# Additions of output parts on GpSimd, ordered behind the scaling of probabilities

## The chip, the core and the metric

The kernel runs on one core of a Trainium2 chip. The metric is device time in microseconds (us) of one execution; less is better. The core has engines that each work through a queue of instructions in order: TensorE (PE; its weight loads are listed apart, as PEld), VectorE (DVE), ScalarE (ACT) and GpSimd (POOL). SyncE (SP) issues DMAs, and so do some of the others.

## The reference

One inference step of a two-layer streaming encoder in fp32, on 1024 prompt tokens and on 8 running streams of 16 new tokens each. Width 1024, 16 query heads of 64 in 4 groups that share a key/value head, MLP width 4096. The first layer's mixer is windowed attention with its own keys and values; the second layer's attends to a shared pair. The change lies in the second, of which the core is:

```python
def attend(q, k, v, bias, sink):                  # sink is None in the second layer
    qg = q.reshape(b, tq, N_KV_HEADS, GROUP, HEAD_DIM)
    s = jnp.einsum('bqhgd,bkhd->bhgqk', qg, k) * (HEAD_DIM ** -0.5)
    s = s + bias.reshape(N_KV_HEADS, GROUP, tq, -1)   # learned bias on clipped distance, band mask
    p = jax.nn.softmax(s, axis=-1)
    return jnp.einsum('bhgqk,bkhd->bqhgd', p, v).reshape(b, tq, N_HEADS * HEAD_DIM)

# second layer, prompt (hp) and running streams (hs) alike
qp = project_q_b(hp, g_attn[layer], w_q_b[j], g_q_b[j])     # RMSNorm, projection, norm of each head
ap = band_attention_prompt(qp, kb_p, vb_p, LEFT_CHUNKS_B, rel_fn, None)  # own chunk of 64 + 8 before
hp = hp + ap @ w_o_b[j]
hp = hp + jnp.square(jax.nn.relu(rmsnorm(hp, g) @ w_up)) @ w_down
```

## The kernel before

**Tiles and halves.** Tokens are cut into tiles of 128: eight of the prompt, numbered 0 to 7, and a ninth, ST, that holds the running streams. The attention of the second layer has two halves: the first takes key/value heads 0 and 1 (query heads 0 to 7) over tiles 0 to 7, the second heads 2 and 3 over the same tiles. One step is a group (tile, key/value head). A float32 matrix product is made of three products of a high and a low part: `split` (L128 to L134) casts the high part and subtracts it to get the low one.

**One group.** A query projection (L217 to L219) reads the normed residual's parts hh and hl from DRAM (hTd), norms and turns it (L238, L239, L260). The scores of a group are stated two groups ahead of its use. PE makes them against up to five tiles of keys (L431; `ps_sf` the far keys, `ps_sn` the near ones), DVE takes minima and adds the bias (L455 to L459), ACT makes the exponentials with their sums (L468, L471), DVE the reciprocals li (L478), and POOL scales each 128x640 row block p by li (L481, two at a time; `score_w` does the same for tiles 2 and 3 at L526). Later PE turns p (L324), ACT and DVE split it into pth and ptl (L128, L134), PE multiplies by the values into `ps_pv` (L331, L332), and `pv_store` copies the result and stores it to DRAM (oTd) in two parts (v = 0 and 1), each of 64 of the 128 rows of `ps_pv`, whose sum is the output.

**Output projection.** `WO(t, half)` (from L1580) brings a tile's output of one half back: `load_halves` loads part 0 into o and part 1 into o2 on SP (L337, L339), and GpSimd adds them in place (L341). Buffers o and o2 come from a scratch pool of two. A split gives oh (cast on POOL, L130) and ol (subtraction on DVE, L134). Then eight pieces of three matmuls each (L176 to L178) go into `ps_mm`, one PSUM bank; DVE adds the residual (L1614), and a DMA stores the tile to xd, on SP's queue for the first half, on POOL's for the second. The pieces are fill work: a plan by hand says at which of the 32 groups a tile's projection is stated, and between the steps of attention a piece at a time is set. Tiles 0 to 5 of the first half are stated at groups 15, 17, 19, 21, 23 and 25, ST at 27, 7 at 28 and 6 at 29; of the second half 0, 4 and 1 at 31, 5, 2 and 3 at 32. These make 14 additions on POOL: eight of the first half, six of the second. The second half of tiles 6, 7 and ST is projected after the attention (`ps_wo`), with the additions on DVE. Tiles 0 and 4 stay in SBUF and are normed there (L641), ordered behind a mark at the last reciprocal. Then come norms, turns of the normed tiles (`ps_n`, L690) and the MLP's matmuls (L743 to L745).

**Decode units.** The running streams' attention is set in small units between the groups (L568 to L615: memset pn, `ps_utp`, `ps_uo`).

**What sets the order.** The code is stated in the order above, and a scheduler then lists every engine's instructions by a model of their times (`TC_KW = dict(schedule_with_timeline_sim=True)`); the engines run those lists in order. So an instruction that is stated early may be listed later on its engine, and with another dependence the list of every engine can come out otherwise. A method adds an order by hand, a dependence on the scheduler's list that is no semaphore:

```python
    def behind(self, a, b):
        self.tc.add_manual_dep(b.ins, a.ins.name, AFTER, reason="order")
```

In the first layer the two parts are not kept apart (its setting `o2` is 0), so it has no such additions.

Of the kernel before, what the change touches and what calls it, by code (L numbers as in the profile page):

```python
# [11 lines left out]
ALU = mybir.AluOpType  # L12
# [82 lines left out]
class Build:  # L95
# [238 lines left out]
    def load_halves(self, layer, half, t, a, b, e=None):  # L334
        nc = self.nc
        src = self.oTd[layer][half][t]
        nc.sync.dma_start(a, src[:, 0])  # L337
        if self.o2[layer] and t < NT:
            nc.sync.dma_start(b(), src[:, 1])  # L339
            e = e or (nc.gpsimd if self.o2[layer] == 1 else nc.vector)  # L340
            e.tensor_tensor(a, a, self.last, ALU.add)  # L341

    def pv_store(self, apool, pv, dst, j):
        nc = self.nc
# [21 lines left out]
    def score_a(self, apool, small, t, j, qT, probs):  # L366
        nc = self.nc
# [6 lines left out]
        p = apool.tile([P, G, 256], F32, tag="p", name="p", bufs=self.pb)  # L374
        for i2 in range(0, G, 2):
# [7 lines left out]
            for i in range(i2, i2 + 2):  # L383
                h = j * G + i
# [8 lines left out]
            for i in range(i2, i2 + 2):  # L393
                h = j * G + i
# [5 lines left out]
                yield  # L400
        li = self.sink_norm(small, nm, self.sink[:, j * G : j * G + G], l, G)
        for i in range(G):
            nc.gpsimd.tensor_scalar(
                p[:, i, 0:W], p[:, i, 0:W], li[:, i : i + 1], 1.0, ALU.mult, ALU.mult
            )
        probs[t, j] = p
# [12 lines left out]
    def score_b(self, apool, small, t, j, qT, probs):  # L419
        nc = self.nc  # L420
# [6 lines left out]
        li = small.tile([P, G], F32, tag="li", name="li")  # L427
# [8 lines left out]
        for i2 in range(0, G, 2):  # L436
# [13 lines left out]
            for i in range(2):  # L450
                h = j * G + i2 + i
# [10 lines left out]
            for i in range(2):  # L462
                h = i2 + i
                p = apool.tile([P, 640], F32, tag="p", name="p", bufs=self.pb)
# [13 lines left out]
            nc.vector.reciprocal(li[:, h2], l[:, h2, 1])  # L478
            for h in range(i2, i2 + 2):
                p = ps[h][:, : nk * P]  # L480
                nc.gpsimd.tensor_scalar(p, p, li[:, h : h + 1], 1.0, ALU.mult, ALU.mult)  # L481
            if i2 == 0:
                yield
        probs[t, j] = ps
# [1 line left out]
    def score_w(self, apool, small, t, j, qT, probs):  # L486
        nc = self.nc
# [6 lines left out]
        li = small.tile([P, G], F32, tag="li", name="li")  # L494
        for i2 in range(0, G, 2):
# [18 lines left out]
            for i in range(2):  # L514
                h = i2 + i
                p = apool.tile([P, 640], F32, tag="p", name="p", bufs=self.pb)
# [6 lines left out]
            nc.vector.reciprocal(li[:, h2], l[:, h2])  # L523
            for h in range(i2, i2 + 2):
                p = ps[h][:, 0:W]
                nc.gpsimd.tensor_scalar(p, p, li[:, h : h + 1], 1.0, ALU.mult, ALU.mult)  # L526
            if i2 == 0:
                yield
        probs[t, j] = ps
# [1376 lines left out]
```

## Time and profile before

| what | value |
|---|---|
| median of 3 runs (lowest, highest) | 2359.23 us (2354.69, 2363.7) |
| the profiled execution: time, span | 2354.01 us, 2352.2 us |
| granted TensorE clock, mean over the span | 0.997 |
| busy: PE, PEld | 2271.4 us (97%), 1893.3 us (80%) |
| busy: DVE, ACT, POOL | 1715.4 us (73%), 1332.4 us (57%), 635.3 us (27%) |

Busy time and spans come from the profile of one execution; the instructions that only issue DMAs or handle semaphores are not counted as busy. In rows of groups, `out<-in` names the tiles, `x14` the count, then busy time, mean ns of one, idle time of the engine just before the group and what ended it. In rows by time the columns are start, duration, engine, line, operation, and in brackets the wait ahead of it and its releaser. A row of waits is engine, tile and line `<-` releaser: us, count, longest. A row of stretches is window, length, busy time with count of PE, PEld, DVE, ACT and POOL, granted clock, busy share of the DMA engines, GB/s. A row of DMA issues ends with KB each and the median us from issue to landing.

### The profile page before, as it was taken

The numbers are of one execution on the slowest core, as the hardware profiler recorded it, in microseconds if no ns is written. First come the engines' busy times: TensorE is split into PE (matmuls) and PEld (weight loads), VectorE is DVE, ScalarE is ACT, GpSimd is POOL, SyncE is SP. The second block draws the span as 40 slices with busy tenths as digits, with TensorE's granted clock in tenths as the row PEclk, the third lists the DMA queues.
The fourth block names the chain that finished last, engine by engine and source line by source line (L and its number), as shares of the span: only waits on it lengthen the run. The fifth ranks groups of instructions, "written<-read, shape, count | busy, mean of one in ns | idle before, by whom it ended". The sixth has DMA issues, their size and how long they took to land.

```text
span 2352.2 us, 33396 instructions
## 1 busy us (share of the span) xinstructions
PE 2271.4 (97%) x11429; PEld 1893.3 (80%) x11429; DVE 1715.4 (73%) x3075; ACT 1332.4 (57%) x2684; POOL 635.3 (27%) x950
## 2 busy tenths in 40 slices
PE   7998999899999999999999999998899999999999
PEld 6787887788888888777877788887788888888787
DVE  6788786766656578899577877777666566678987
ACT  3777674655555555344377666665655555565443
POOL 4334332313213111002333434344132132110011
PEclk9999999999999999999999999999999999999999
DMA  7335546234434677748653655555244343977567
GB/s 253 127 113 163 171 147 202 95 122 160 137 111 151 218 230 177 267 147 214 183 157 113 193 157 177 174 168 184 69 156 138 113 162 107 284 209 199 175 169 192
DMA packets 226715, 392.70 MB, mean 167 GB/s; under 512 B 51592, under 2 KB 126288, under 8 KB 226448
## 3 DMA queue, kind: packets, MB, share of 16 engines
q1 hardware_dynamic: 188816, 283.58, 37.4%
q0 software_dynamic: 36432, 102.26, 15.9%
q10 hardware_dynamic: 1296, 4.72, 0.5%
q8 instruction: 90, 1.47, 0.2%
q14 instruction: 81, 0.66, 0.1%
HBM read 236.51 MB, written 156.85 MB: 167 GB/s over the span
## 4 chain that ended last, share of the span: by engine, by line
PE 74%; DVE 9%; DMA 9%; ACT 3%; issue 3%; POOL 1%; SPq 0%; ACTq 0%; DVEq 0%; POOLq 0%
PE ps_c L743 6%; PE ps_c L744 6%; PE ps_c L745 6%; PE ps_x L743 5%; PE ps_x L745 5%; PE ps_x L744 5%; PE ps_mm L217 3%; PE ps_mm L219 3%; PE ps_mm L218 3%; PE ps_y L745 2%; PE ps_y L743 2%; PE ps_y L744 2%; PE ps_tr L324 2%; DMA a<-hd 2%; DVE w L134 1%
## 5 line engine op out<-in xcount | busy, mean ns | idle before, releaser
L744 PE MATMUL ps_c<-w,a 128*128 128x512 f32 x960 | 374.7, 390 | 6.9 <-DVE w L134 6.9
L743 PE MATMUL ps_c<-w,a 128*128 128x512 f32 x960 | 375.1, 391 | 5.1 <-DVE x L1174 3.1
L745 PE MATMUL ps_c<-w,a 128*128 128x512 f32 x960 | 374.3, 390 | 0.0
L908 POOL DMA_DIRECT2D hd<-h x272 | 148.9, 550 | 594.8 <-ACT h L817 378.2
L743 PEld LDWEIGHTS ps_c<-w,a 128*128 128x128 f32 x960 | 180.6, 188 | 46.3 <-issue 4.7
L744 PEld LDWEIGHTS ps_c<-w,a 128*128 128x128 f32 x960 | 180.7, 188 | 46.1 <-DVE w L134 9.0
L745 PEld LDWEIGHTS ps_c<-w,a 128*128 128x128 f32 x960 | 180.5, 188 | 37.5
L128 ACT CAST a<-a 128x1536 fp32r<-128x1536 f32 x80 | 118.6, 1482 | 149.5 <-DMA a<-hd 149.5
L217 PE MATMUL ps_mm<-w,hh 128*128 128x512 f32 x432 | 172.7, 401 | 8.8 <-POOL w L185 3.3
L134 DVE TENSOR_TENSOR a<-a 128x1536 fp32r<-128x1536 f32 x80 | 140.5, 1756 | 45.7 <-ACT a L128 45.7
L219 PE MATMUL ps_mm<-w,hl 128*128 128x512 f32 x432 | 171.7, 398 | 1.5 <-DMA hl<-hTd 1.4
L218 PE MATMUL ps_mm<-w,hh 128*128 128x512 f32 x432 | 170.8, 396 | 1.3 <-DVE w L190 1.1
L743 PE MATMUL ps_x<-sx,w 128*128 128x512 f32 (+1 forms) x408 | 157.8, 387 | 3.7 <-ACT h L864 2.7
L128 ACT CAST w<-s 128x2048 fp32r<-128x2048 f32 x56 | 107.1, 1912 | 92.2 <-DVE s L1060 80.7
L128 ACT CAST w<-ru 128x512 fp32r<-128x512 f32 (+1 forms) x160 | 110.0, 708 | 83.9 <-PE ps_y L744 32.0
L745 PE MATMUL ps_x<-sx,w 128*128 128x512 f32 (+1 forms) x408 | 154.1, 378 | 0.0
L744 PE MATMUL ps_x<-sx,w 128*128 128x512 f32 (+1 forms) x408 | 154.1, 378 | 0.0
L134 DVE TENSOR_TENSOR w<-s,w 128x2048 fp32r<-128x2048 f32 x56 | 128.1, 2288 | 32.4 <-ACT w L128 32.3
L1179 POOL DMA_DIRECT2D xp<-o x28 | 36.3, 1296 | 411.8 <-ACT o L1162 390.2
L134 DVE TENSOR_TENSOR ptl<-ps_tr,pth 128x512 fp32r<-128x512 f32 x180 | 122.4, 685 | 24.1 <-ACT pth L128 18.2
L134 DVE TENSOR_TENSOR w<-ru,w 128x512 fp32r<-128x512 f32 (+1 forms) x160 | 126.6, 793 | 14.7 <-ACT w L128 14.6
L816 ACT ACTIVATE h<-h 128x512 f32<-128x512 f32 (+1 forms) x102 | 61.9, 607 | 122.6 <-DVE h L866 93.5
(274 smaller groups left out, 6131.4 us busy)
## 6 DMA issues: line engine op xcount, KB each, us to landing
a<-hd SPq DMA_DIRECT2D x80, 768.0 KB, 6.2
hd<-h POOLq DMA_DIRECT2D x272, 192.0 KB, 2.5
ru<-in_w_up SPq DMA_DIRECT2D x64, 512.0 KB, 3.9
r<-in_w_down SPq DMA_DIRECT2D x32, 1024.0 KB, 10.0
xp<-o POOLq DMA_DIRECT2D x28, 768.0 KB, 9.4
o<-oTd SPq DMA_DIRECT2D x50, 256.0 KB, 5.0
x<-xp SPq DMA_DIRECT2D x23, 512.0 KB, 5.2
xp<-xo SPq DMA_DIRECT2D x18, 512.0 KB, 2.8
```

Of the source, the lines that this page charges most:

```text
L128: a = nc.scalar.copy(hi, src)
L134: return a, e.tensor_tensor(lo, src, hi.bitcast(F32), ALU.subtract)
L217: nc.tensor.matmul(ps, a, w[:, 0, k, :], start=(k == 0), stop=False)
L218: nc.tensor.matmul(ps, a, w[:, 1, k, :], start=False, stop=False)
L219: self.lp = nc.tensor.matmul(ps, b, w[:, 0, k, :], start=False, stop=(k == KC - 1))
L324: self.lp = nc.tensor.transpose(pt[:, i, :], get(i), self.ident)
L743: a = mm(ps, ah, bh, start=first, stop=False, skip_group_check=True)
L744: mm(ps, ah, bl, start=False, stop=False, skip_group_check=True)
L745: return a, mm(ps, al, bh, start=False, stop=last, skip_group_check=True)
L816: a = nc.scalar.activation(t, src, AF.Relu)
L908: return lambda p, z: self.nc.gpsimd.dma_start(self.hd[c // 4][:, p, c % 4], z)
L1179: nc.gpsimd.dma_start(dst, z, accum_op=ALU.add)
```

## The change

`load_halves` orders the addition behind `self.pl` where it is on GpSimd and of the first half. `self.pl` is the scaling of probabilities stated last: the three loops that scale on GpSimd set it. Eight additions are tied so (tiles 0 to 7 of the first half); the six of the second half on GpSimd and those on DVE are not. The scheduler then lists all engines anew.

```diff
@@ load_halves
         if self.o2[layer] and t < NT:
             nc.sync.dma_start(b(), src[:, 1])
-            e = e or (nc.gpsimd if self.o2[layer] == 1 else nc.vector)
-            e.tensor_tensor(a, a, self.last, ALU.add)
+            if e is None and not half:
+                self.behind(self.pl, nc.gpsimd.tensor_tensor(a, a, self.last, ALU.add))
+            else:
+                (e or nc.gpsimd).tensor_tensor(a, a, self.last, ALU.add)
...
@@ score_b (score_a and score_w alike)
             for h in range(i2, i2 + 2):
                 p = ps[h][:, : nk * P]
-                nc.gpsimd.tensor_scalar(p, p, li[:, h : h + 1], 1.0, ALU.mult, ALU.mult)
+                self.pl = nc.gpsimd.tensor_scalar(p, p, li[:, h : h + 1], 1.0, ALU.mult, ALU.mult)
```

From L342 on, line numbers of the changed kernel are two higher. Both kernels hold the same instructions. The lists are alike up to the first addition on POOL and again from the first matmuls of the second layer's MLP.

POOL's list around the first addition (tile 0), before:

```order
L481 TENSOR_SCALAR p_13624<-p_13624,li_13552 128x640
L481 TENSOR_SCALAR p_13627<-p_13627,li_13552 128x640
L341 TENSOR_TENSOR o_14133<-o_14133,o2_14135 128x512
L130 CAST oh_14138<-o_14133 128x512
L481 TENSOR_SCALAR p_13785<-p_13785,li_13766 128x640
L481 TENSOR_SCALAR p_13788<-p_13788,li_13766 128x640
L583 MEMSET pn_14096 128x128
L238 TENSOR_TENSOR qrs_14322<-qms_14320,mhalf_68 128x8
L481 TENSOR_SCALAR p_13847<-p_13847,li_13766 128x640
```

and in the changed kernel:

```order
L483 TENSOR_SCALAR p_13959<-p_13959,li_13940 128x640
L483 TENSOR_SCALAR p_13962<-p_13962,li_13940 128x640
L483 TENSOR_SCALAR p_14019<-p_14019,li_13940 128x640
L483 TENSOR_SCALAR p_14022<-p_14022,li_13940 128x640
L341 TENSOR_TENSOR o_14133<-o_14133,o2_14135 128x512
L585 MEMSET pn_14473 128x128
L130 CAST oh_14138<-o_14133 128x512
L483 TENSOR_SCALAR p_14176<-p_14176,li_14157 128x640
L483 TENSOR_SCALAR p_14179<-p_14179,li_14157 128x640
L238 TENSOR_TENSOR qrs_14322<-qms_14320,mhalf_68 128x8
```

The addition stood behind p_13627 and stands behind p_14022 now; the eight scalings from p_13785 to p_14022 have moved ahead of it.

PE's list where the projection of tile 0 begins (the first row with oh), before:

```order
L260 MATMUL ps_q<-identr,qr 128x128 x4
L431 MATMUL ps_sn<-KT,qT 128x256 x4
L331 MATMUL ps_pv<-pth,VS 128x512
L332 MATMUL ps_pv<-ptl,VS 128x512
L324 MATMUL ps_tr<-identr,p 128x128 x4
L331 MATMUL ps_pv<-pth,VS 128x512
L176 MATMUL ps_mm<-w,oh 128x512
L177 MATMUL ps_mm<-w,oh 128x512
L178 MATMUL ps_mm<-w,ol 128x512
```

and in the changed kernel:

```order
L331 MATMUL ps_pv<-pth,VS 128x512
L324 MATMUL ps_tr<-identr,p 128x128 x4
L332 MATMUL ps_pv<-ptl,VS 128x512
L260 MATMUL ps_q<-identr,qr 128x128 x4
L331 MATMUL ps_pv<-pth,VS 128x512
L176 MATMUL ps_mm<-w,oh 128x512
L177 MATMUL ps_mm<-w,oh 128x512
L332 MATMUL ps_pv<-ptl,VS 128x512
L324 MATMUL ps_tr<-identr,p 128x128 x4
L331 MATMUL ps_pv<-pth,VS 128x512
L433 MATMUL ps_sn<-KT,qT 128x128 x4
L178 MATMUL ps_mm<-w,ol 128x512
```

43 more matmuls of attention stand ahead of the projection, and the first one that needs ol stands apart from those that need oh.

PE's list at the end of the attention, from the last product `ps_pv` on, before:

```order
L331 MATMUL ps_pv<-pth,VS 128x512
L332 MATMUL ps_pv<-ptl,VS 128x512
L605 MATMUL ps_utp<-identr,ub 128x128
L606 MATMUL ps_utp<-identr,ub 128x128
L607 MATMUL ps_utp<-identr,pn 128x128
L690 MATMUL ps_n<-identr,xo 128x128 x8
L613 MATMUL ps_uo<-pts,vc 64x128
L614 MATMUL ps_uo<-pts,vc 64x128
L615 MATMUL ps_uo<-pts,v_11138 64x128
L690 MATMUL ps_n<-identr,xo 128x128 x4
L176 MATMUL ps_wo<-w,oh 128x512
```

and in the changed kernel:

```order
L331 MATMUL ps_pv<-pth,VS 128x512
L332 MATMUL ps_pv<-ptl,VS 128x512
L607 MATMUL ps_utp<-identr,ub 128x128
L608 MATMUL ps_utp<-identr,ub 128x128
L609 MATMUL ps_utp<-identr,pn 128x128
L692 MATMUL ps_n<-identr,xo 128x128 x8
L615 MATMUL ps_uo<-pts,vc 64x128
L616 MATMUL ps_uo<-pts,vc 64x128
L617 MATMUL ps_uo<-pts,v_11138 64x128
L692 MATMUL ps_n<-identr,xo 128x128 x4
L176 MATMUL ps_mm<-w,oh 128x512
```

Where the projections of the wo phase (`ps_wo`) followed, pieces of the attention's own projections (`ps_mm`) follow now: 36 of their matmuls come after the last product.

4 lines of the change are left out of this document (2 added, 2 removed).

## The prediction

> **What bounds the kernel now.** The page comes first: TensorE is busy for nearly the whole span, and most of the chain that ended last is its work.
>
> ```profile
> span 2352.2 us, 33396 instructions
> PE 2271.4 (97%) x11429; PEld 1893.3 (80%) x11429; DVE 1715.4 (73%) x3075; ACT 1332.4 (57%) x2684; POOL 635.3 (27%) x950
> ...
> PE 74%; DVE 9%; DMA 9%; ACT 3%; issue 3%; POOL 1%; SPq 0%; ACTq 0%; DVEq 0%; POOLq 0%
> ```
>
> POOL has 1% of that chain. The listed order of instructions differs between the two kernels only from POOL's first addition of the second attention up to the first matmuls of its MLP, and both hold the same instructions. So I cut the view by stretches there: the first runs from that point to the last probability-times-value product, the second from there to the MLP. The columns are busy time and count for PE, PEld, DVE, ACT and POOL.
>
> ```profile
> 1357.00:1612.00 255.00, 248.68 (x1384) 208.23 (x1382) 193.06 (x525) 163.80 (x458) 107.04 (x148) 1.00 0.55 171
> 1612.00:1668.00 56.00, 44.44 (x259) 36.36 (x259) 44.09 (x63) 31.63 (x60) 26.45 (x21) 0.94 0.40 133
> ```
>
> PE is idle 255.00 - 248.68 = 6.3 us in the first and 56.00 - 44.44 = 11.6 us in the second. No reordering can gain more than the sum, 17.9 us, 0.76% of the span. The view of waits gives their causes; the first two rows are PE's largest in the first stretch (after them come single waits of at most 1.0), the last is PE's largest in the second.
>
> ```profile
> PE ps_pv L332 <- DVE ptl L134: 1.9, 3, 1.2
> PE ps_sf L431 <- ACT p L468: 1.0, 2, 0.6
> ...
> PE ps_n L690 <- DVE sx L134: 8.7, 8, 2.4
> ```
>
> No row of either answer names POOL. POOL's own groups, from the view by lines in 1340 to 1612 us, say what the change touches:
>
> ```profile
> L341 POOL TENSOR_TENSOR o<-o,o 128x512 f32<-128x512 f32 x14 | 18.0, 1286 | 33.9 <-DMA o<-oTd 29.4 <-DVE li L478 4.4
> ```
>
> The 14 additions keep POOL waiting 29.4 us for loads, and the scalings queued behind them wait as long. But POOL is busy only 107.04 of 255.00 us, and PE, which reads the scaled probabilities, never waits for it: the scores run two groups ahead.
>
> **The change part by part.** Nothing is computed anew. What goes is POOL's waiting in front of scalings: worth nothing on PE by the rows above, bounded by 0 and 6.3 us, and I take 0, because no row of PE names a scaling. What comes is an order: the eight additions of the first half (tiles 0 to 7) stand behind the scaling stated last, so the output projection that needs the sum hangs on a score chain and no longer on a load alone.
>
> The first addition stood between the scalings of p_13627 and p_13785 and stands behind p_14022 now. When was p_14022 scaled? In time order POOL reads:
>
> ```profile
> 1354.79 1.30 POOL L341 TENSOR_TENSOR o<-o,o 128x512 f32<-128x512 f32 x1 [3.04 <-DMA o<-oTd]
> ...
> 1378.76 1.58 POOL L481 TENSOR_SCALAR p<-p,li 128x640 f32<-128x640 f32 x2 [6.68 <-DVE ps_sf L455]
> 1380.36 0.61 POOL L130 CAST oh<-o 128x512 fp32r<-128x512 f32 x1
> 1381.53 0.20 POOL L583 MEMSET pn<- 128x128 f32 x1 [0.56 <-PE ps_utp L607]
> ```
>
> The row at 1378.76 is p_14019 and p_14022. Their reciprocal on DVE ended at 1378.6:
>
> ```profile
> 1376.61 0.69 DVE L1614 TENSOR_TENSOR xo<-ps_mm,xo 128x512 f32<-128x512 f32 x1
> ...
> 1378.43 0.16 DVE L478 RECIPROCAL li<-l 128x2 f32<-128x2 f32 x1
> ```
>
> In DVE's new order the projection's own sum (0.69) and one multiplication (0.69, row below) no longer stand ahead of that reciprocal, so it can come about 1.3 us earlier, near 1377.3. Then follow two scalings (1.58), the addition (1.30), a memset (0.20) and the cast (0.61): oh is ready at 1377.3 + 3.7 = 1381.0. DVE's subtraction for ol, before it PE can go on, stands behind three minima of far scores, three biased minima and two splits, and is a third such split. At the prices of these groups that is 1.65 + 1.47 + 2.05, with about 1 us of small ones 6.2: ol is ready at about 1383.5.
>
> ```profile
> L134 DVE TENSOR_TENSOR ptl<-ps_tr,pth 128x512 fp32r<-128x512 f32 x83 | 56.3, 684 | 10.4 <-ACT pth L128 5.5 <-PE ps_pv L332 4.1
> L456 DVE TENSOR_REDUCE mnb<-ps_sf 128x1 f32<-128x384 f32 x44 | 23.8, 548 | 0.5
> L459 DVE CUSTOM_DVE_ANT_0 ps_sn<-ps_sn,biasB,mnb 128x256 f32<-128x256 f32 x46 | 22.5, 490 | 1.1
> ```
>
> When does PE ask? Before, it began that projection at 1372.38, twelve matmuls in 2.76 us:
>
> ```profile
> 1370.69 0.71 PE L431 MATMUL ps_sn<-KT,qT 128*128 128x256 f32 x4
> 1371.24 0.40 PE L331 MATMUL ps_pv<-pth,VS 128*128 128x512 f32 x1
> ...
> 1372.38 0.40 PE L176 MATMUL ps_mm<-w,oh 128*128 128x512 f32 x1
> ...
> 1375.14 0.39 PE L332 MATMUL ps_pv<-ptl,VS 128*128 128x512 f32 x1
> ...
> 1375.86 0.51 PE L431 MATMUL ps_sf<-KT,qT 128*128 128x384 f32 x2
> 1376.21 0.40 PE L332 MATMUL ps_pv<-ptl,VS 128*128 128x512 f32 x1
> ```
>
> Now 43 more matmuls of attention stand ahead of it: six products at 0.23, two of a decode unit in 0.26, four pairs of far scores at 0.35, two sets of near scores at 0.5 and 19 transposes at 0.1, together 6.1 us. (From the starts above: 1371.24 to 1372.38 are three products and four transposes, 1375.14 to 1375.86 two products and the unit's two.) PE asks for oh at 1378.5 and, 1.8 us of work later, for ol at 1380.3; it gets ol at 1383.5. **Wait here: 3.2 us.** It lies on PE's path, so it is loss at this place. The bounds are 0 (DVE catches up) and 3.2 + 1.3 = 4.5 (the reciprocal comes no earlier than it did).
>
> For the other additions I counted PE's work, at the same prices, between the last scores of the scaling ahead and the projection. At the first place the near scores began at 1370.69 and the scalings ended at 1380.3; addition, cast and subtraction add 2.6, so 12.2 us are needed. Later it is shorter:
>
> ```profile
> 1526.89 0.69 PE L431 MATMUL ps_sn<-KT,qT 128*128 128x256 f32 x4
> ...
> 1532.65 1.58 POOL L481 TENSOR_SCALAR p<-p,li 128x640 f32<-128x640 f32 x2
> ```
>
> These are 7.3 and 2.6, 9.9 us. Two projections (tiles 7 and 6) have 10.0 us of PE work in between, the other five 15.8 to 17.7. The two lie near the second row in the program, so I take 0 for them; the bound by the first row is 2.2 each, 4.4. The shift also moves what the additions hold: the scratch buffers, hence the next query projection, its loads on SP (hh, hl) and the residual's store and load. Between one query projection's last matmul and the next one's first, PE work was 10.9 to 12.2 us and is now 12.6 to 14.6; a load of hh or hl lands in 4 to 5 us, so it stays hidden.
>
> ```profile
> hh<-hTd SPq DMA_DIRECT2D x17, 512.0 KB, 4.2
> hl<-hTd SPq DMA_DIRECT2D x17, 512.0 KB, 5.0
> ```
>
> A rule of the Trainium skill speaks against the move. The row first: a DVE multiplication of two SBUF operands took 0.69 us alone and 1.12 while POOL scaled.
>
> ```profile
> 1374.10 0.69 DVE L239 TENSOR_TENSOR qr<-qr,qrs 128x512 f32<-128x512 f32 x1
> ...
> 1396.41 1.12 DVE L239 TENSOR_TENSOR qr<-qr,qrs 128x512 f32<-128x512 f32 x1
> ```
>
> The Trainium skill, "SBUF — State Buffer", section "Who interferes with whom", says that a DVE instruction with two SBUF inputs contends with a GpSimd instruction that reads SBUF; by that rule and these rows, eight additions set beside such work would cost 8 x 0.43 = 3.4 us of DVE. I count none: the number of additions and of DVE instructions is unchanged.
>
> The end of the stretch gains. Before, all projections of the attention were done when the last product ran; now 36 of their matmuls (at 0.23, 8.3 us) come after it. So the last product, the last decode unit and the norms of the kept tiles that are ordered behind it come 8.3 - 3.2 = 5.1 us earlier, and PE has 8.3 us more to do where it waited 11.6. What ends that tail is read from these rows:
>
> ```profile
> 1611.64 2.46 DVE L641 SCALAR_TENSOR_TENSOR xo<-xo,mrs,gb 128x1024 f32<-128x1024 f32 x2
> ...
> 1627.77 0.39 PE L178 MATMUL ps_wo<-w,ol 128*128 128x512 f32 x1
> ...
> 1630.82 1.29 DVE L681 TENSOR_TENSOR x<-ps_wo,x 128x512 f32<-128x512 f32 x2 [1.59 <-DMA x<-xp]
> ...
> 1639.09 2.28 DVE L641 SCALAR_TENSOR_TENSOR x<-x,mrs,gb 128x1024 f32<-128x1024 f32 x1
> ```
>
> The path through the kept norms (1611.64) moves by -5.1. The path through tile 7, whose projection ended at 1628.2, moves by -5.1 + 8.3 = +3.2, to 1631.4; its sum waited for a load until 1630.8, so its own delay is 0.6. The path through tile 3, projected last, has its projection 15.6 us of PE work later:
>
> ```profile
> 1607.41 0.69 DVE L1614 TENSOR_TENSOR xo<-ps_mm,xo 128x512 f32<-128x512 f32 x1 [0.99 <-PE ps_mm L178]
> ...
> L636 ACT ACTIVATE junk<-x 128x1024 bf16<-128x1024 f32 x7 | 7.4, 1058 | 0.3 <-DMA x<-xp 0.3
> xp<-xo POOLq DMA_DIRECT2D x9, 512.0 KB, 3.2
> x<-xp SPq DMA_DIRECT2D x23, 512.0 KB, 5.2
> ```
>
> Its sum starts at 1607.4 + 15.6 + 3.2 = 1626.2; with 0.7 for it, 3.2 for the store, 5.2 for the load, 1.1 for the square and 2.3 for the scaling the norm ends at 1638.7, where the row at 1639.09 ended at 1641.4: no delay. The tail's end is set by the first two in turn, so I take their middle, -2.2, about **-2 us**. Both ends stay: -8.3 if no new wait arises, 4.5 + 4.4 = +8.9 if every wait has its upper bound and the tail absorbs nothing. After the stretch the order is the same, PE is full, and the shift passes to the end one to one.
>
> The profiled execution took 2354.0 us, 1.8 beyond its span; the change makes that 2352. The median of the runs shown, 2359.23, lies 5.2 above it, so on the median I predict 2357, with 2351 to 2368 as this case's own range (-8.3 and +8.9).
>
> **The rivals.** *PE starves at every addition (slower).* The mechanism is the one priced at 3.2 us. If DVE's backlog stretches the score chain beyond the 15.8 us that five projections have, all eight wait. For it: between DVE's splits for ptl_14067 and ptl_14343 (1374.7 to 1400.3 in the trace) PE's work falls from 25.2 to 16.5 us, while DVE's stays what it is in this row, 20.82:
>
> ```profile
> 1374.00:1401.00 27.00, 27.00 (x152) 22.91 (x151) 20.82 (x66) 17.05 (x56) 9.20 (x13) 1.00 0.61 183
> ```
>
> Against it: DVE is busy 193.06 of 255.00 in the whole stretch, and further on the fill between attention work is displaced, not missing. Price: 8 x 3.2 = 25.6, less the 5.2 that the tail gives back in my case (from +3.2 to -2): +20, 2379. From six waits on (19.2 - 5.2 = 14) it is slower by 0.5%. Chance 0.20, a tenth of it milder than that.
>
> *POOL was the hidden brake (faster).* If PE's busy time hides waiting, freeing POOL shows. For it: PE's weight loads are busy 208.23 of 255.00, 82%. Of the loads' 29.4 us, 16.6 belong to the eight tied additions (the first at 1354.79 above, the last here); if they come off, 2342.
>
> ```profile
> 1514.21 1.29 POOL L341 TENSOR_TENSOR o<-o,o 128x512 f32<-128x512 f32 x1 [1.98 <-DMA o<-oTd]
> ```
>
> Against it: matmuls of 512 columns follow each other at 0.23 us all through (2.76 for twelve), so there is no slack between them, and no wait of PE names POOL. The Trainium skill, "Perfetto Trace Analysis", section "Identifying the Most-Contended Engine", holds matmul busy time to be no good measure and names weight-load busy time instead; by that rule the stretch has 18% to give. Chance 0.10.
>
> That the additions do not move is ruled out by the listed order.
>
> **How the numbers follow.** My case has 0.70, the slower rival 0.20, the faster 0.10. About 0.5% (11.8 us) is what a measurement of this kernel can tell from no change. My case lies within it; so faster 0.10, same 0.72, slower 0.18. The range reaches from 2346, into the faster rival, to 2372, into the milder part of the slower one, and leaves out about 2 in 10.
>
> **What would show it.** Right: POOL's additions wait little for oTd, PE shows a wait of some 3 us at L176 to L178 near 1380, PE's idle time in the second stretch falls below 10 us, and the MLP's first long run of matmuls starts within 5 us of before. Wrong: waits of PE for oh or ol, or for DVE splits, that come again with each tile (the slower rival); or an idle share of PE in the first stretch that is unchanged with a stretch shorter by over 10 us (the faster one).

## The result and the profile after

| | median of 21 runs each (lowest, highest) | profiled execution: time, span, granted clock |
|---|---|---|
| before | 2358.30 us (2351.61, 2364.68) | 2354.01, 2352.2, 0.997 |
| after | 2364.39 us (2358.94, 2368.46) | 2362.41, 2360.6, 0.992 |

The ratio is 1.0027, with a 95% interval of 1.0019 to 1.0034: the changed kernel is some 6 us slower, where 2 us less had been forecast. The runs lie inside the range given; the direction was wrong.

The same two stretches as before the change, from the view by stretches of the changed kernel, with the first 43 us apart. This execution was 3.2 us late before it reached anything that differs (the last copy `vsb` on ACT, L282, ahead of the change started at 1316.09, in before at 1312.88), so its windows begin at 1360.40 where those of before begin at 1357.00.

```profile
1360.40:1403.40 43.00, 39.25 (x232) 31.50 (x231) 35.09 (x107) 31.48 (x96) 18.98 (x29) 1.00 0.43 126
1360.40:1612.00 251.60, 243.17 (x1357) 202.39 (x1356) 189.43 (x520) 164.56 (x461) 107.27 (x147) 1.00 0.52 163
1612.00:1678.75 66.75, 53.64 (x288) 44.02 (x287) 50.16 (x69) 31.33 (x59) 27.96 (x24) 0.90 0.47 150
```

And the first 43 us of before:

```profile
1357.00:1400.00 43.00, 42.41 (x252) 36.03 (x251) 34.41 (x100) 29.78 (x86) 17.03 (x21) 1.00 0.56 166
```

PE was idle 43.00 - 42.41 = 0.6 us in the first 43 us and is idle 3.75 now: +3.2 us, the size forecast. In the whole attention it is idle 8.4 us (6.3 before). The second stretch is where the time went: from the last product `ps_pv` to the first activation of the MLP (L816 before, L818 after). These are the two windows cut exactly so, before and then after, each from the view by stretches.

```profile
1611.50:1665.35 53.85, 42.45 (x238) 34.04 (x238) 43.59 (x64) 30.69 (x59) 26.45 (x21) 0.94 0.38 128
```
```profile
1610.79:1676.09 65.30, 52.35 (x275) 42.47 (x273) 50.42 (x70) 31.04 (x58) 27.96 (x24) 0.90 0.45 146
```

Below this stretch is called the seam. It grew by 11.4 us. PE has 9.9 us more work there (8.3 forecast), and its idle time did not shrink: 53.85 - 42.45 = 11.4 before, 12.95 now. DVE got 6.8 us more work.

What PE waited for, changed kernel, view of waits in 1360 to 1404 us, then in 1612 to 1680 us:

```profile
PE ps_sf L433 <- ACT p L470: 1.4, 3, 0.6
PE ps_pv L332 <- DVE ptl L134: 1.2, 3, 0.8
PE ps_utp L607 <- ACT ub L603: 0.8, 1, 0.8
PE ps_pv L331 <- ACT pth L128: 0.4, 1, 0.4
...
PE ps_n L692 <- DVE sx L134: 9.9, 7, 2.4
```

In the first place PE waits for the attention's own chains: for exponentials p, for the split parts ptl and pth, and for ub of a decode unit. No row names oh or ol. That these waits show because no projection is left there to fill them is argued, not shown. The first projection began at 1387.85, behind its listed neighbours, from PE's rows by time:

```profile
1387.53 0.48 PE L331 MATMUL ps_pv<-pth,VS 128*128 128x512 f32 x1
1387.85 0.39 PE L176 MATMUL ps_mm<-w,oh 128*128 128x512 f32 x1
...
1389.62 0.44 PE L178 MATMUL ps_mm<-w,ol 128*128 128x512 f32 x1
```

POOL's additions, from its groups in 1340 to 1612 us: the eight tied ones (L341) wait 0.6 us, the six others 17.9. Before, all 14 had waited 33.9.

```profile
L341 POOL TENSOR_TENSOR o<-o,o 128x512 f32<-128x512 f32 x8 | 10.3, 1286 | 0.6 <-DMA o<-oTd 0.6
...
L343 POOL TENSOR_TENSOR o<-o,o 128x512 f32<-128x512 f32 x6 | 7.9, 1311 | 17.9 <-DMA o<-oTd 17.9
```

The seam on DVE, changed kernel, by time. L1616 is the sum behind an attention projection (here the second half of tiles 2 and 3), L643 a norm, L683 the sum behind a projection of the wo phase.

```profile
1612.50 0.68 DVE L1616 TENSOR_TENSOR xo<-ps_mm,xo 128x512 f32<-128x512 f32 x1
1613.10 1.91 DVE L643 SCALAR_TENSOR_TENSOR x<-x,mrs,gb 128x1024 f32<-128x1024 f32 x1
...
1616.70 0.69 DVE L1616 TENSOR_TENSOR xo<-ps_mm,xo 128x512 f32<-128x512 f32 x1 [1.10 <-PE ps_mm L178]
...
1627.28 1.27 DVE L643 SCALAR_TENSOR_TENSOR x<-x,mrs,gb 128x1024 f32<-128x1024 f32 x1
1628.47 0.68 DVE L1616 TENSOR_TENSOR xo<-ps_mm,xo 128x512 f32<-128x512 f32 x1
...
1636.67 1.28 DVE L643 SCALAR_TENSOR_TENSOR x<-x,mrs,gb 128x1024 f32<-128x1024 f32 x1 [1.96 <-DMA xp<-x]
...
1637.93 0.68 DVE L1616 TENSOR_TENSOR xo<-ps_mm,xo 128x512 f32<-128x512 f32 x1
...
1655.42 0.14 DVE L640 TENSOR_SCALAR mms<-mssq 128x1 f32<-128x1 f32 x1
1655.48 1.27 DVE L683 TENSOR_TENSOR x<-ps_wo,x 128x512 f32<-128x512 f32 x2
1656.67 1.27 DVE L134 TENSOR_TENSOR sx<-ps_n,sx 128x512 fp32r<-128x512 f32 x2
1657.87 1.27 DVE L643 SCALAR_TENSOR_TENSOR x<-x,mrs,gb 128x1024 f32<-128x1024 f32 x1
```

All these sums of before came ahead of its last product, and so did the norms of tiles 1 and 5 (1613.10 and 1627.28 here; in before:)

```profile
1589.84 1.28 DVE L641 SCALAR_TENSOR_TENSOR x<-x,mrs,gb 128x1024 f32<-128x1024 f32 x1
...
1603.27 1.28 DVE L641 SCALAR_TENSOR_TENSOR x<-x,mrs,gb 128x1024 f32<-128x1024 f32 x1
```

Tile 3's last sum is the one at 1637.93. Its last matmul had started at 1632.01; the sum stands in DVE's list behind the norm at 1636.67, and that norm (of tile 6), which works in place, waited for the store of its own tile to finish. Then come POOL's store of tile 3, SP's reload of it, the square on ACT and the norm at 1657.87. POOL's, SP's and ACT's rows, each from its engine's rows by time:

```profile
1639.83 0.60 POOL L1618 DMA_DIRECT2D xp<-xo  x1
```
```profile
1627.96 0.80 SPq L662 DMA_DIRECT2D x<-xp  x2
1628.80 15.00 SPq L773 DMA_DIRECT2D ru<-in_w_up  x3
1643.90 1.41 SPq L662 DMA_DIRECT2D x<-xp  x2
```
```profile
1652.27 1.06 ACT L638 ACTIVATE junk<-x 128x1024 bf16<-128x1024 f32 x1
```

The two loads at 1643.90 are those of tiles 3 and ST; they stand on SP behind loads of w_up that held the queue for 15.00 us. Most of that was itself a wait for tile 3's store, as SP's own waits in 1610 to 1666 us show:

```profile
SPq L773 <- DMA xp<-xo: 12.6, 1, 12.6
```

ST's sum is the row at 1655.48; in DVE's list it stands behind tile 3's mean square at 1655.42. That mean square did not hold it up: DVE's rows show no wait from 1646.69 to there, only work. The waits of DVE in the seam, first before, then after (largest first):

```profile
DVE sx L134 <- ACT sx L128: 4.6, 4, 2.2
DVE o L341 <- DMA oh<-oTd: 1.8, 1, 1.8
```
```profile
DVE mms L640 <- ACT junk L638: 4.3, 2, 3.3
DVE x L643 <- DMA xp<-x: 4.1, 2, 2.1
DVE o L343 <- DMA oh<-oTd: 2.6, 1, 2.6
```

The new ones are for squares on ACT and for stores of tiles that are normed in place. Before had 0.2 of the first and none of the second.

The chain that ended last, as the profile follows it back (changed kernel, view of that chain, 1600 to 1682 us), does not pass through tile 3's store and reload. It takes tile 7's second sum, the store of tile 7, the norm that waited for this store, DVE's work to 1655.57, turns and first MLP matmuls on PE, and ST's norm, the last one:

```profile
1642.17 0.61 DVE x L683
1642.80 3.80 DMA xp<-x
1646.69 0.13 DVE x L643
...
1661.26 2.24 DVE x L643
```

This is one execution, and its releasers are inferred.

### The profile page after: what moved, and what is told of

It reads as the page before. It is cut to its first block, busy times and chain, and to the rows that moved or that the text cites. A ratio compares the mean times of both kernels' runs of the same rounds, so it can differ in the third digit from the quotient of the medians.

```text
span 2360.6 us, 33391 instructions
## 1 busy us (share of the span) xinstructions
PE 2278.2 (97%) x11429; PEld 1899.2 (80%) x11429; DVE 1718.2 (73%) x3075; ACT 1332.8 (56%) x2684; POOL 636.5 (27%) x950
## 4 chain that ended last, share of the span: by engine, by line
PE 78%; DVE 7%; DMA 7%; ACT 4%; issue 2%; POOL 1%; SPq 0%; ACTq 0%; DVEq 0%; POOLq 0%
PE ps_c L746 8%; PE ps_c L745 8%; PE ps_c L747 8%; PE ps_x L745 5%; PE ps_x L746 5%; PE ps_x L747 5%; PE ps_mm L217 3%; PE ps_mm L219 3%; PE ps_mm L218 3%; PE ps_y L747 2%; PE ps_y L745 2%; PE ps_y L746 2%; DMA a<-hd 2%; PE ps_tr L324 2%; PE ps_mm L176 1%
## 5 line engine op out<-in xcount | busy, mean ns | idle before, releaser
L134 DVE TENSOR_TENSOR w<-s,w 128x2048 fp32r<-128x2048 f32 x56 | 128.1, 2287 | 33.9 <-ACT w L128 33.8
L818 ACT ACTIVATE h<-h 128x512 f32<-128x512 f32 (+1 forms) x102 | 61.9, 607 | 122.1 <-DVE h L868 93.1
```

Of the source, the lines that this page charges most:

```text
L134: return a, e.tensor_tensor(lo, src, hi.bitcast(F32), ALU.subtract)
L818: a = nc.scalar.activation(t, src, AF.Relu)
```

## The experiments

Theory A: the ties' waits in the attention cost the time. Theory B: the projections left over to the seam cost it, by where they stand among those of the wo phase. The ratio is to the kernel before, run on the same chip beside it, with its 95% interval. The other columns are from one profile of each, in us from the start of the last `vsb` copy ahead of the change. One profile scatters by nearly as much as the loss in question: the changed kernel and e9_after3c, whose PE lists differ in the place of one matmul, differ by 3.6 us in the last column, and before and e18_before_nostores, whose lists are the same on every engine up to the last product, differ by 4.6 us at that product. So only the ratios decide.

| run | ratio [95%] | last product | last left-over projection | first activation |
|---|---|---|---|---|
| before | 1 | 298.6 | 294.1 (none left over) | 352.5 |
| after | 1.0027 [1.0019, 1.0034] | 294.7 | 315.9 | 360.0 |
| e1_tie67 | 1.0040 [1.0026, 1.0054] | 304.1 | 328.7 | 370.0 |
| e2_tie0 | 0.9995 [0.9986, 1.0005] | 296.3 | 309.6 | 351.2 |
| e3_late36 | 1.0014 [1.0001, 1.0026] | 299.1 | 314.6 | 357.0 |
| e4_front | 1.0003 [0.9990, 1.0015] | 293.5 | 308.7 | 352.7 |
| e5_late24 | 1.0007 [0.9994, 1.0020] | 296.9 | 304.1 | 355.4 |
| e6_keep3 | 1.0035 [1.0021, 1.0048] | 295.9 | 316.8 | 361.1 |
| e7_twice | 1.0020 [1.0008, 1.0032] | 296.7 | 318.4 | 361.3 |
| e8_no23 | 1.0001 [0.9989, 1.0013] | 295.0 | (none left over) | 353.2 |
| e9_after3c | 1.0034 [1.0020, 1.0047] | 294.0 | 315.3 | 356.4 |
| e10_after4 | 1.0014 [1.0001, 1.0027] | 297.2 | 318.6 | 361.0 |
| e11_before4 | 0.9990 [0.9974, 1.0005] | 296.8 | (none left over) | 349.0 |
| e12_tie0front4 | 0.9998 [0.9986, 1.0009] | 299.3 | 307.6 | 355.2 |
| e13_nostore3 | 1.0026 [1.0014, 1.0037] | 296.9 | 318.1 | 361.0 |
| e14_before_no23 | 0.9991 [0.9982, 1.0001] | 291.7 | (none left over) | 351.5 |
| e15_before_no23x4 | 1.0002 [0.9991, 1.0013] | 295.0 | (none left over) | 353.9 |
| e16_prev4 | 1.0029 [1.0018, 1.0040] | 303.8 | 303.4 (none left over) | 361.9 |
| e17_after_nostores | 1.0025 [1.0013, 1.0036] | 296.4 | 317.5 | 359.7 |
| e18_before_nostores | 0.9995 [0.9986, 1.0004] | 303.2 | (none left over) | 355.0 |

**Parts of the change alone.** e1_tie67 ties only tiles 7 and 6, e2_tie0 only tile 0, both in the changed kernel:

```diff
-            if e is None and not half:
+            if e is None and not half and t > 5:     # e1_tie67;   e2_tie0: and t == 0
```

> Only the additions of tiles 7 and 6 are tied; those of tiles 0 to 5 stand where they stood before. PE's list is that of before until tile 7's projection, and after the last product it is nearly that of the changed kernel: the same 36 matmuls of tiles 2 and 3 are left over there, spread between the projections of the wo phase. Measure: the stretch from the last ACT cast that both kernels have in common ahead of the change to the first ReLU of the second MLP, 350.0 us before and 357.5 in the changed kernel (+7.5). Theory 'seam' (what is lost is lost behind the last product, by projections that come late and hold up the stores, loads and norms of tiles 5, 2 and 3): no wait near the first projection, stretch +4 to +8, time +3 to +8 us over before. Rival 'first projection' (the loss comes from the 3.2 us that PE waits near tile 0's projection, and what follows is its echo): stretch and time within 1.5 us of before.

> Only the addition of tile 0 is tied. PE waits about 3 us near tile 0's projection as in the changed kernel; 24 matmuls (tile 3's) are left over behind the last product instead of 36. Theory 'seam': stretch +2 to +6, less than the changed kernel's +7.5, because a third of the late projections is gone. Rival 'first projection': stretch +7 to +8, all of the changed kernel's loss.

e2_tie0 has the first tie and with it the wait of 3.6 us, from its view by stretches:

```profile
1359.70:1402.70 43.00, 39.37 (x229) 31.53 (x228) 34.59 (x105) 30.09 (x93) 18.52 (x29) 1.00 0.44 127
```

The total does not show it: 0.9995. So theory A fails for the place at which the forecast put its 3.2 us. e1_tie67, without that place, costs as much as the whole change or more, 9 us or so, and more than the 3 to 8 us that were expected. Its left-over projections end later than in any other run, and PE is idle 5.0 us in the stretch below (its view by stretches), where before is idle 2.5 and after 1.2.

```profile
1500.00:1550.00 50.00, 45.02 (x245) 36.64 (x244) 39.32 (x107) 36.28 (x102) 15.14 (x21) 0.90 0.41 122
```

**Left-over projections alone.** e3_late36 and e5_late24 take the kernel before and order its last 36 or last 24 projection matmuls behind the last product; nothing is tied on POOL.

```diff
+            if self.fence is not None:
+                self.behind(self.fence, a)          # a: the first matmul of a piece
...
+                    self.fence = self.lastpv if layer and half and (t == 3 or (t == 2 and n)) else None   # e5: t == 3 alone
                     self.wo_proj(ps, oh, ol, wo[half], nn, [k])
```

> The kernel before, no addition tied, with one order added: the last 36 matmuls of the attention's projections (tile 2's second half, tile 3) are put behind the last product. POOL's list is that of before up to there. Theory 'seam': stretch +5 to +9 over before without any tied addition, the norms of tiles 5, 2 and 3 late as in the changed kernel. Rival 'first projection': within 2 us of before. Rival 'cover' (the matmuls that leave the attention's end uncover waits there): PE idle in the last 40 us ahead of the last product up by 4 us or more, and no more than 2 us lost behind it.

> As the kernel with 36 matmuls put behind the last product, but with tile 3's 24 alone. From the runs so far, counted from the last vsb copy ahead of the change: tile 3's last projection matmul and the MLP's first ReLU stood at 294.1 and 352.5 us (before), 309.6 and 351.2 (tile 0 tied), 308.7 and 352.7 (left-over ones in one piece), 314.6 and 357.0 (36 put behind), 315.9 and 360.0 (changed kernel), 328.7 and 370.0 (tiles 7 and 6 tied). Theory 'tile 3's path' (its sum, store, load, norm and turns take some 42 us to the first ReLU, with about 15 us of slack in the kernel before): last matmul near 308 to 310, first ReLU at 350 to 353, time within 2 us of before. Rival 'each matmul behind the last product costs its own time': 24 x 0.23 = 5.5 us, ReLU near 358.

36 of them cost 0.14% (3 us, interval 0.2 to 6), 24 nothing that can be told. So left-over projections cost time without any tie, but whether it is nearly none or nearly all of the loss, this interval leaves open. In e3_late36 24 of the 36 run ahead of the wo phase's matmuls and 12 among them; in the changed kernel 12 run ahead and 24 among them. e2_tie0 has 12 ahead and 12 among them, at no loss.

**Where they stand.** e4_front is the changed kernel with the wo phase's projections ordered behind the last of the attention's, in one piece. e8_no23 takes the second half of tiles 2 and 3 out of the attention's plan, so that the wo phase projects them.

```diff
+            self.fence = self.lw if layer else None        # e4_front; lw: the last matmul of L178
...
-  32: [('B', 5), ('B', 2), ('B', 3)]
+  32: [('B', 5)]                                           # e8_no23
```

> The changed kernel, with one order added: every projection matmul of the wo phase (tiles 6, 7, ST) stands behind the last of the 36 left over, which so come in one piece, tile 3's last near 1625 instead of 1632 us in the profile. Theory 'seam by interleaving' (tile 3's late sum, store and load set the MLP's start): stretch shorter than the changed kernel's by 4 to 7 us. Rival 'amount' (8.3 us of work stand on PE's path behind the last product, in whatever order): within 1.5 us of the changed kernel.

> The changed kernel, with the second half of tiles 2 and 3 left out of the attention's plan: the wo phase projects them, as it does tiles 6, 7 and ST, with their additions on DVE and without a store and load between sum and norm. No projection of the attention is left over behind the last product, and 48 matmuls more stand in the wo phase. Theory 'tile 3's path': first ReLU at 348 to 354, time 5 us or more below the changed kernel. Rival 'amount' (11 us of projection behind the last product are 11 us later, whatever their path): 360 or more.

Each takes the loss away (1.0003 and 1.0001, intervals apart from that of after). "In one piece" means with no matmul of the wo phase between; turns of normed tiles still stand there. In e4_front all ties are there, the last product comes as early as in after, and PE's seam holds the same 275 matmuls; the seam from its view by stretches:

```profile
1608.07:1667.23 59.16, 49.10 (x275) 40.78 (x273) 48.21 (x70) 31.35 (x59) 27.27 (x24) 0.94 0.48 161
```

59.16 us against 65.30, with the same instruction counts on PE and DVE. Tile 3's last sum is at 1625.65 there (1637.93 in after), and SP's rows by time show the reloads of tiles 3 and ST at 1634.37 and 1635.42 (1643.90 in after), 8 us earlier when the two executions are counted from their common start (1314.55 and 1316.09):

```profile
1625.98 8.28 SPq L778 DMA_DIRECT2D ru<-in_w_up  x2
1634.37 0.48 SPq L666 DMA_DIRECT2D x<-xp  x1
1634.90 0.42 SPq L778 DMA_DIRECT2D ru<-in_w_up  x1
1635.42 0.46 SPq L666 DMA_DIRECT2D x<-xp  x1
```

Of the 8.28 us, 7.4 were again a wait for tile 3's store. The chain that ended last follows PE's matmuls here, from 1620.57 to 1643.69.

**Which link of the seam.** Five attempts to cut one link of the changed kernel. e7_twice does the turns of the wo phase twice, which keeps PE's clock up; e6_keep3 keeps tile 3 in SBUF, with no store and reload of it; e10_after4 gives the reloads a fourth buffer x, for which one buffer o and the squares' scratch (its edit is not shown) had to move, so e9_after3c has those moves alone, and e11_before4 is the kernel before with all of it; e13_nostore3 leaves out tile 3's store on top of e10_after4, and e17_after_nostores the stores of tiles 6, 7 and ST in the wo phase (e18_before_nostores the same from before).

```diff
-                for k in range(4):
+                for k in list(range(4)) * (2 if layer else 1):            # e7_twice
...
-  xt={..., ('B', 2): 'hh', ('B', 3): 'hl'}
+  xt={..., ('B', 2): 'hh', ('B', 3): 'keep'}                              # e6_keep3
...
-                o = work.tile([P, 4, P], F32, tag=f"o{z}", name="o")
+                o = work.tile([P, 4, P], F32, tag="o" if layer else f"o{z}", name="o")     # e9, e10, e11, e13
...
-                    xs[t] = work.tile([P, D], F32, tag="x", name="x", bufs=3)
+                    xs[t] = work.tile([P, D], F32, tag="x", name="x", bufs=4 if layer else 3)  # e10, e11, e13
...
+                            if not (layer and half and t == 3):           # e13: no store of tile 3
...
-                if t not in self.wo_done:
+                if t not in self.wo_done and not layer:                   # e17, e18: no store
                     nc.scalar.dma_start(self.xd[t], x)
```

> The changed kernel; each turn of a normed tile in the second wo phase is made twice (the second overwrites the first with the same), 4 more transposes of 0.1 us in each of some 30 turns, most of them where PE waits. Theory 'cold clock' (PE's waits at the seam bring the granted clock to 0.5 in three stretches, against one before, and this is 2 to 3 of the 7.5 us): less cold time, first ReLU 1 to 3 us earlier than 360. Rival 'path' (turns lie on the path and the clock follows the waits without costing much): 360 to 364.

> The changed kernel, with tile 3's second sum kept in SBUF like those of tiles 0 and 4: its norm needs no load of what was just stored (12.4 us from the store's issue at 1639.83 to the square at 1652.27 in the changed kernel). Its projection stands where it stands in the changed kernel. Theory 'tile 3's path': last matmul near 316 as there, first ReLU at 350 to 355, so 5 to 10 us earlier than in the changed kernel. Rival 'tile 5's path' (its load on SP's queue behind the last products' stores, its norm 20 us late): 358 to 361, as there.

> Control for the next one: the changed kernel with, in the second wo phase, one buffer for the loaded o instead of two and the squares' unused output written into the last MLP operand's tile. Three buffers x, as in the changed kernel; PE's list is that of the changed kernel. Every theory: first ReLU at 358 to 362 us after the last vsb copy, time within 2 us of the changed kernel.

> The control with a fourth buffer x in the second wo phase. In the profiles so far tile 3's x is loaded into the buffer of tile 1, and ST's into that of tile 5; the two loads leave at 1631.1 and 1635.8 us before and at 1643.9 and 1645 in the changed kernel, each right after the last reader of the buffer (GpSimd's fourth sum for tiles 1 and 5 ended at 1631.1 before; the turns of tiles 1 and 5 at 1643.6 in the changed kernel), and the first ReLU comes 28 to 37 us after the last of the two in all ten profiles. Theory 'buffers' (the left-over projections delay the turns of tiles 1 and 5, these the loads of tiles 3 and ST, these the MLP): with a fourth buffer tile 3's load waits only for its store and ST's for tile 1's readers: first ReLU 4 to 8 us before the control's. Rival 'tile 3's store' (it lands near 1643 anyway): within 1.5 us of the control. Rival 'turn order' (PE's list itself): the same.

> The kernel before, with the fourth buffer x (and the one buffer o, the squares' output as in the control). No addition is tied, nothing is left over. Theory 'buffers': the loads of tiles 3 and ST leave 5 to 15 us earlier than at 1631.1 and 1635.8, first ReLU at 345 to 350 against 352.5, time 2 to 7 us under before. Rival: the seam of the kernel before is bound by something else (PE and DVE are both busy 80% of it): within 1.5 us.

> The changed kernel with the fourth buffer x, and without the store of tile 3's second sum (so tile 3's x in the wo phase lacks the second half's projection). PE's list is nearly that of the changed kernel, tile 3's projection as late. Theory 'tile 3's store': in the changed kernel SP's second w_up load waits for that store until 1642.86, and the loads of tiles 3 and ST go behind it (1643.9); DVE's sum for ST stands behind tile 3's mean square. Without the store the load of tile 3's x stands ahead of w_up and leaves some 15 us earlier, DVE's sums for ST come near 330 instead of 339 us after the last vsb copy, first ReLU at 350 to 355, time within 2 us of the kernel before. Rival 'PE's list' (the interleaved projections delay tiles 6, 7 and ST whatever tile 3 does): 357 to 361, 3 to 8 us over before.

> The changed kernel without the stores of tiles 6, 7 and ST in the second wo phase (so the MLP's residual of these tiles lacks the second half's projection). Their norms overwrite the tile in place and so waited for these stores, 4.1 us of DVE's waiting there. Theory 'DVE at the seam' (the change moved 6.8 us of DVE work behind the last product and added 4 to 5 us of waits in its list, and DVE has no idle time there): DVE's waiting 4 us less, first ReLU at 354 to 357, time +1 to +4 us over before. Rival 'PE's list': 359 to 362, +5 to +8 us.

> The kernel before without the same stores. No norm waited for a store there (0 us), so theory 'DVE at the seam' expects no more than the scatter: first ReLU at 350 to 354, time within 2 us of before. Rival 'the stores' traffic' (they slow the loads of the seam): 3 us or more under before, and as much as in the changed kernel.

None brings the time back beyond its interval. In e7_twice the clock stays at 1.00 all through the seam, from its view by stretches,

```profile
1613.71:1678.33 64.62, 58.46 (x395) 51.37 (x393) 48.83 (x70) 31.96 (x59) 28.83 (x24) 1.00 0.47 156
```

and the seam is as long (64.62 against 65.30), the ratio 1.0020. So a full clock alone does not bring the time back. That the half clock costs nothing is not shown: the doubled turns add 6.1 us of PE's busy time (58.46 against 52.35), which can hide what the clock gives. e6_keep3 stays at 1.0035, but is confounded: without tile 3 in the row, the reloads of tiles 7 and ST came late (1642.59 and 1653.61), after waits of 17.1 us together for turns on PE. The fourth buffer is unclear (1.0014 against 1.0034 for its control, overlapping intervals). Leaving out tile 3's store (1.0026) or the stores that the in-place norms wait for (1.0025, and 0.9995 from before) does not bring it back either, though tile 7's store lies on the chain shown above; without the stores that chain still runs through DVE's list.

**Both sides.** e12_tie0front4 joins the harmless tie, the one piece and the fourth buffer; e14_before_no23 is the kernel before with e8_no23's edit, e15_before_no23x4 with the fourth buffer as well.

> Tile 0's addition alone tied, the projections of the wo phase ordered behind the 24 left over, and the fourth buffer x. Theory 'buffers': the last product stands at 293 to 296 us as with tile 0 tied (before: 298.6), and the seam can use what it gives: first ReLU at 344 to 349, time 4 to 8 us under before. Rival (seam bound by the work on PE and DVE): 350 to 353.

> The kernel before, untied, with tiles 2 and 3's second half left to the wo phase. Theory 'tile 3's store' and its round trip through DRAM: attention shorter by most of 11 us of projection, the seam longer by about as much less what its waits can hide (11.4 us of PE idle there before): first ReLU at 347 to 352, time 0 to 5 us under before. Rival 'cover' (the end of the attention waits without these matmuls as fill, as with the 36 put behind): 352 to 356, no gain.

> The same with the fourth buffer x (one buffer o, the squares' output as in the control). If the x buffers also hold up the seam, first ReLU 2 to 4 us before the run without it, 344 to 349, time 3 to 7 us under before; if not, the same as that run.

None is faster than before by more than its interval. The lowest, e11_before4 and e14_before_no23, reach 0.9990 and 0.9991 with intervals that hold 1; joined in e15 they give 1.0002. The theory that the buffers x hold up the seam had expected e12_tie0front4 4 to 8 us and e15_before_no23x4 3 to 7 us under before; it fails.

**A run that theory B does not cover.** e16_prev4 ties all eight additions, but to the scaling stated four earlier. Then nothing is left over to the seam.

```diff
-                self.behind(self.pl, nc.gpsimd.tensor_tensor(a, a, self.last, ALU.add))
+                self.behind(self.pq[-1 - 4], nc.gpsimd.tensor_tensor(a, a, self.last, ALU.add))   # pq: all scalings
```

> The eight additions tied, but behind the scaling stated four earlier (one half group further back). PE's list moves less: nothing is left over behind the last product. Theory 'left-over projections': within 2 us of before, first ReLU at 350 to 354, though GpSimd waits less for loads at its additions. Rival 'hidden brake' (GpSimd's waiting costs PE time): 3 us or more under before. Rival 'the tie itself': 3 us or more over before.

It costs 0.29% all the same. In this one profile the attention is 5.2 us longer than that of before (last product 303.8 against 298.6), the seam 4.2. Neither says where the loss lies: e18_before_nostores has its last product at 303.2 and no loss. PE's waits in its attention, largest first, are small; the last one, for POOL, has no like in before:

```profile
PE ps_pv L332 <- DVE ptl L134: 2.0, 4, 1.3
PE ps_utp L609 <- ACT ub L605: 1.5, 2, 0.8
PE ps_pv L331 <- ACT pth L128: 1.2, 2, 0.8
PE ps_tr L324 <- POOL p L485: 1.1, 1, 1.1
```

So left-over projections are one way to lose these microseconds and not the only one: a re-listing with no left-over cost as much, and where it did is not shown. With that, a rival stays open: that the changed kernel, too, loses part of its time to something else in its new lists.

## Why the prediction was wrong, point by point

- *POOL's waits for loads are worth nothing on PE*: right. The tied additions wait 0.6 us, and PE gained nothing in the attention. The rival in which POOL was the hidden brake is refuted by PE's idle time there (8.4 us, not less than 6.3).
- *A wait of 3.2 us at the first projection*: right in place, wrong in kind, and its size (PE idle +3.2 us) right by luck. It was foreseen for oh and ol; it came at the far scores, at ptl and at ub. The sum behind it is also slightly off: its parts make 5.9 us and not 6.1. e2_tie0 has this wait and no loss.
- *No wait at the other seven additions*: right for after, whose attention waits 2.1 us more in all. The rival in which PE starves at every addition (+20 us) is refuted. In e1_tie67 PE idles 5.0 us in the 50 us ahead of its second tied addition (at 1551.72), but in waits for ub, p, pth and ptl, none for oh or ol.
- *The last product comes 5.1 us earlier*: 3.9 by the start counted above, which one profile cannot tell from 5.1. The direction holds: in the eight profiles of kernels with all ties and the left-over projections of after it lies at 293.5 to 297.2, in the two with the list of before at 298.6 and 303.2.
- *The seam takes in 8.3 us of moved matmuls, PE's idle time falls below 10 us, and the path through tile 3 has no delay*: this is the step that failed. PE's idle time rose from 11.4 to 12.95, the MLP's first activation came 7.5 us later in the profile, and the time rose by some 6 us against a forecast of -2. Two terms were missing. With the 36 matmuls went other work of the same tiles: three sums, and two norms of tiles 1 and 5 listed near them; DVE's busy time in the seam rose by 6.8 us. And the path through tile 3 was summed as if each step could start when its input is there. Its last matmul came 21.8 us later than in before, against 18.8 forecast. From the last matmul of the projection to the sum the forecast had next to nothing; the trace has 1637.93 - 1632.01 = 5.9 us, behind a norm that waited for a store. From the store's issue to the square it had 8.4 us (3.2 and 5.2); the trace has 1652.27 - 1639.83 = 12.4. Counted from the same start, tile 3's sum was forecast for 313.3 and came at 321.8, its norm's end for 325.8 and came at 343.0. ST's norm, the last one in both kernels, ended later still, at 347.4 (337.9 in before); the forecast had no path through ST.
- *If the tail absorbs nothing, up to +8.9*: this bound held the result.
- *About 0.5% is what a measurement can tell*: too coarse; 21 runs each told 0.27% with an interval of 0.19 to 0.34%.

What is shown: the time of the change is lost between the last product and the MLP, and it comes back when the left-over projections stand in one piece or are made in the wo phase (e4_front, e8_no23); 36 of them there cost some 3 us without any tie (e3_late36). What is argued only: that the loss runs through DVE's fixed order of sums, norms and splits. The rows above show its new waits, the chain that ended last in the changed kernel runs through that order and not through tile 3's store and reload, and the sums of tile 3 are late in every slower run with left-overs (at 315 to 332 from the start above, 307 to 311 in e2, e4, e5 and e12). But no single link, taken away, brought the time back, so several chains of nearly equal length may end together there. Which one must be shortened stays open, and so does the cost of e16_prev4.

## What to carry to other kernels

When a re-listing pushes fill work of one engine past the end of a stage, count what goes with it on the other engines (sums, norms, stores, reloads) and where these now stand in their fixed lists; the sum of durations along one tile's path is only a lower bound. Idle time of the busiest engine at a seam is not free room: here 9.9 us more of PE's work met 11.4 us of idle time and none of it was absorbed, while the same matmuls in one piece cost nothing that could be told. A wait of the busiest engine at one place need not show in the total, as e2_tie0 has it. And one profile of each kernel does not place a loss of a few microseconds: here two kernels with the same lists differ by 4.6 us at the end of the same stage.

## What the runs showed of the hardware

Three things. The granted clock fell to about half after stretches in which PE had little to do. From the view by stretches of the changed kernel, the sparse stretch and the one behind it, and PE's longest wait ahead of the fall:

```profile
1648.00:1652.00 4.00, 1.93 (x12) 1.26 (x12) 4.00 (x6) 1.38 (x3) 2.50 (x2) 0.93 0.88 328
1651.00:1657.00 6.00, 4.12 (x19) 3.43 (x20) 6.00 (x9) 3.10 (x6) 3.89 (x4) 0.54 0.05 21
```
```profile
1648.72 1.23 PE L692 MATMUL ps_n<-identr,s 128*128 128x128 f32 x8 [1.84 <-DVE sx L134]
```

The Trainium skill, "TensorE: Matmul & The Clock Gate", section "What's actually happening", has half the clock after an idle window of about 3.4 us. The half agrees; a gap of that length does not stand in the trace, where PE was busy about half of the sparse stretch and waited 1.84 us at most. The rule against idle gaps above about 3.4 us, in the same page of the Trainium skill, section "HAM oscillation — how this bites in real kernels", is not settled here: in e7_twice the clock stayed full and the time did not move beyond its interval.

One queue held others up for long: three loads of w_up took SP 15.00 us in after and two of them 8.28 in e4_front, with the reloads of the last tiles behind them. Of these, 12.6 and 7.4 us were a wait of the loads for a store, and not the issuing.

And DVE's norm of one 128x1024 tile took 1.27 us where POOL did nothing beside it (1627.28 and 1657.87 in after) and 1.91 to 2.29 us where POOL was adding on such tiles at the same time (1613.10, 1638.68 and 1661.22).
